# An instance normalization rewritten with one program per engine, an on-chip loop over six slots, a halved last tile and an early short write

## The chip, the cores and the metric

The kernel runs on one core of a Trainium2 chip. A core has a matrix engine (PE), a vector engine (DVE), a scalar engine (ACT), GpSimd (POOL), a sequencer that only issues and waits (SP), and 16 DMA engines that they share. The metric is the device time of one execution in microseconds (us), the median over several runs. The profile of one run gives a span about 1.8 us shorter than that time (1247.6 us against 1249.35 us here), because it counts from the first to the last instruction.

## The reference

```python
def reference(x, eps):           # x: (8, 64, 32, 64, 64) float32, standard normal
    mean = np.mean(x, axis=(2, 3, 4), keepdims=True)
    var = np.var(x, axis=(2, 3, 4), keepdims=True)
    return ((x - mean) / np.sqrt(var + eps)).astype(np.float32)
```

There are 512 instances of 131,072 elements. 268.4 MB are read and 268.4 MB written.

## The kernel before

It is written in a tile framework, which inserts the waits and allocates the semaphores. A tile is 128 partitions by 8192 elements, 4 MB, and holds eight instances, each spread over 16 partitions; there are 64 tiles and six buffers. SP loads, ACT stores.

```python
    def load(g):
        t = data_pool.tile([P, F], fp32, name="xt")          # bufs=6
        nc.sync.dma_start(out=t, in_=x_t[g])
        return t

    def compute(t):
        cut = F // 2
        nc.vector.reduce_sum(out=sums[:, 0:1], in_=t[:, :cut], ...)             # L83
        nc.scalar.activation(out=unused[:, cut:], in_=t[:, cut:],               # L86
                             func=Act.Identity, accum_out=sums[:, 1:2])
        nc.tensor.matmul(out=mean_ps, lhsT=avg, rhs=sums, ...)   # sum over 16 partitions
        nc.vector.tensor_reduce(out=neg_mean, in_=mean_ps, negate=True, ...)
        nc.scalar.activation(out=unused, in_=t, func=Act.Square,                # L103
                             bias=neg_mean, accum_out=squares)
        nc.tensor.matmul(out=var_ps, lhsT=avg, rhs=squares, ...)
        nc.scalar.activation(out=std, in_=var_ps, func=Act.Sqrt, bias=eps_t)
        nc.vector.reciprocal(out=scale, in_=std)
        nc.vector.tensor_mul(out=bias, in0=neg_mean, in1=scale)
        nc.vector.tensor_scalar(out=t[:, cut:], ...)             # x*scale+bias, L114
        nc.scalar.activation(out=t[:, :cut], ...)                # the same,    L122
    # ... cut ...
        for g in range(n_tiles):
            t = load(g)
            compute(t)
            nc.scalar.dma_start(out=out_t[g], in_=t)             # L131
```

## Time and profile before

| | value |
|---|---|
| time, median (first three runs) | 1249.35 us (1249.16 to 1250.83) |
| DMA rate in the middle of the run | 433 GB/s |
| 536.9 MB at that rate | about 1240 us |
| ACT busy, DVE busy | 77%, 37% |

The first lines are the head of the page of the kernel before, its DMA slices (each digit is the busy tenths of a fortieth of the span), its DMA queues (q1 carries the loads, q10 the stores, q14 and q8 instruction fetches) and its DMA issues (the last number is the median time from issue to landing).

```profile
span 1247.6 us, 1828 instructions
PE 73.6 (6%) x256; PEld 64.2 (5%) x256; DVE 467.4 (37%) x322; ACT 961.6 (77%) x386; POOL 0.9 (0%) x6
...
DMA  9999999999999999999999999999999999999998
...
q14 instruction: 9, 0.07, 0.0%
q8 instruction: 2, 0.03, 0.0%
...
xt<-in_x_dram SPq DMA_DIRECT2D x64, 4096.0 KB, 53.3
out_dram<-xt ACTq DMA_DIRECT2D x64, 4096.0 KB, 45.2
```

The DMA engines are busy throughout. A 4 MB tile takes 9.7 us at 433 GB/s if nothing else moves, and a load and a store together take 19.4 us. That transfers need 45 to 53 us to land therefore means that two to three of each kind are always queued. A compute step of a middle tile, which takes ACT about 17.5 us, is hidden.

The windows view of the kernel before gives, for each stretch of the span, its length, the busy time and number of instructions of PE, PE weight loads, DVE, ACT and POOL, the granted clock, the DMA share and the rate in GB/s.

```profile
20.00:40.00 20.00, 1.17 (x4) 1.00 (x4) 7.22 (x5) 18.10 (x8) 0.00 (x0) 1.00 1.00 416
40.00:1200.00 1160.00, 69.58 (x242) 60.68 (x242) 444.97 (x304) 910.77 (x366) 0.00 (x0) 1.00 1.00 433
...
1232.00:1234.00 2.00, 0.00 (x0) 0.00 (x0) 0.00 (x0) 1.15 (x1) 0.00 (x0) 1.00 0.34 147
1234.00:1243.00 9.00, 0.00 (x0) 0.00 (x0) 0.00 (x0) 0.00 (x0) 0.00 (x0) 1.00 1.06 455
1243.00:1246.00 3.00, 0.00 (x0) 0.00 (x0) 0.00 (x0) 0.00 (x0) 0.00 (x0) 1.00 0.15 66
```

For 93% of the span the rate is 433 GB/s. What can be gained lies in the edges: some 416 GB/s where the first store joins, a dip at 1233 us, and a last stretch in which only a few DMA engines still work (share 0.15). The timeline of the kernel before (start, duration, engine, line, what, and in brackets the idle time before it) shows where the dip comes from:

```profile
0.81 75.23 SPq L77 DMA_DIRECT2D xt<-in_x_dram  x8
...
13.07 3.62 ACT L86 ACTIVATE unused<-xt 128x4096 uint8<-128x4096 f32 x1 [10.99 <-DMA xt<-in_x_dram]
...
31.60 0.37 ACTq L131 DMA_DIRECT2D out_dram<-xt  x1
...
1213.72 0.34 ACTq L131 DMA_DIRECT2D out_dram<-xt  x1
...
1229.35 3.80 ACT L122 ACTIVATE xt<-xt,bias,scale 128x4096 f32<-128x4096 f32 x1 [0.47 <-DVE bias L113]
1233.18 0.34 ACTq L131 DMA_DIRECT2D out_dram<-xt  x1
```

The last store can be issued only at 1233.18, about when the store before it, issued at 1213.72, runs dry.

### The profile page before, as it was taken

What the parts mean: (1) busy time and instruction counts of PE and PEld (TensorE: products, weight loads), DVE (VectorE), ACT (ScalarE), POOL (GpSimd) and SP (SyncE); (2) the same over time, 40 slices, a digit from 0 to 9 for tenths busy, and PEclk for the clock granted to TensorE, in tenths of its full rate; (3) what the DMA queues carried; (4) which work ended last, traced back from release to release, by engine and by line L of the source; (5) the groups of instructions that cost most, each with busy time, mean ns of one, the idle gap of its engine ahead of it and who ended that gap; (6) DMA issues with size and microseconds to landing.
All of it is one profiled execution on the core that took longest, in us unless ns stands there. A gap on an engine that the chain in (4) does not pass through costs nothing.

```text
span 1247.6 us, 1828 instructions
## 1 busy us (share of the span) xinstructions
PE 73.6 (6%) x256; PEld 64.2 (5%) x256; DVE 467.4 (37%) x322; ACT 961.6 (77%) x386; POOL 0.9 (0%) x6
## 2 busy tenths in 40 slices
PE   0000000000000000000000000000000000000000
PEld 0000000000000000000000000000000000000000
DVE  2344433433334334343343433434334333343331
ACT  5888888787777877778777777777787777877774
POOL 0000000000000000000000000000000000000000
DMA  9999999999999999999999999999999999999998
GB/s 403 420 437 434 434 427 436 435 435 427 435 436 434 434 428 435 435 434 427 437 435 434 433 429 437 435 432 427 437 436 434 429 431 435 436 434 425 437 436 364
DMA packets 18443, 536.99 MB, mean 430 GB/s; under 512 B 2048, under 2 KB 2048, under 8 KB 2048
## 3 DMA queue, kind: packets, MB, share of 16 engines
q1 hardware_dynamic: 9216, 268.44, 49.9%
q10 hardware_dynamic: 9216, 268.44, 49.8%
q14 instruction: 9, 0.07, 0.0%
q8 instruction: 2, 0.03, 0.0%
HBM read 268.44 MB, written 268.44 MB: 430 GB/s over the span
## 4 chain that ended last, share of the span: by engine, by line
ACT 45%; DVE 32%; another core or an unknown queue 12%; PE 6%; issue 2%; DMA 1%; ACTq 0%
ACT unused L103 37%; DVE sums L83 19%; DVE xt L114 10%; ACT xt L122 4%; ACT unused L86 3%; PE var_ps L107 3%; PE mean_ps L93 3%; ACT std L109 1%; DMA xt<-in_x_dram 1%; DVE scale L111 1%; DVE neg_mean L95 1%; DVE bias L113 1%; ACTq L131 0%; ACT L109 0%
## 5 line engine op out<-in xcount | busy, mean ns | idle before, releaser
L103 ACT ACTIVATE unused<-xt,neg_mean 128x8192 uint8<-128x8192 f32 x64 | 455.8, 7121 | 100.6 <-DVE neg_mean L95 100.6
L83 DVE TENSOR_REDUCE sums<-xt 128x1 f32<-128x4096 f32 x64 | 282.8, 4419 | 167.6 <-DMA xt<-in_x_dram 167.6
L86 ACT ACTIVATE unused<-xt 128x4096 uint8<-128x4096 f32 x64 | 231.5, 3617 | 96.1 <-DMA xt<-in_x_dram 91.5
L122 ACT ACTIVATE xt<-xt,bias,scale 128x4096 f32<-128x4096 f32 x64 | 243.3, 3801 | 31.3 <-DVE bias L113 31.3
L111 DVE RECIPROCAL scale<-std 128x1 f32<-128x1 f32 x64 | 10.5, 164 | 530.8 <-ACT std L109 530.8
L114 DVE TENSOR_SCALAR xt<-xt,scale,bias 128x4096 f32<-128x4096 f32 x64 | 154.4, 2413 | 2.7 <-DVE bias L113 0.3
L93 PE MATMUL mean_ps<-sums,avg 128*128 128x2 f32 x128 | 36.0, 351 | 670.9 <-DVE sums L83 573.9
L93 PEld LDWEIGHTS mean_ps<-sums,avg 128*128 128x128 f32 x128 | 32.1, 311 | 674.7 <-ACT unused L86 657.1
L107 PE MATMUL var_ps<-squares,avg 128*128 128x1 f32 x128 | 37.6, 363 | 484.1 <-ACT unused L103 484.1
L107 PEld LDWEIGHTS var_ps<-squares,avg 128*128 128x128 f32 x128 | 32.1, 312 | 489.6 <-ACT unused L103 489.6
L109 ACT ACTIVATE std<-var_ps,eps_t 128x1 f32<-128x1 f32 x64 | 16.7, 261 | 42.7 <-PE var_ps L107 42.7
L95 DVE TENSOR_REDUCE neg_mean<-mean_ps 128x1 f32<-128x2 f32 x64 | 10.2, 160 | 60.1 <-PE mean_ps L93 60.1
L103 ACT ACTIVATION_READ_ACCUMULATOR unused<-xt,neg_mean 128x1 f32 x64 | 11.9, 187 | 0.0
L86 ACT ACTIVATION_READ_ACCUMULATOR unused<-xt 128x1 f32 x64 | 11.9, 186 | 0.0
L113 DVE TENSOR_TENSOR bias<-neg_mean,scale 128x1 f32<-128x1 f32 x64 | 10.2, 160 | 2.2
L86 ACT ACT_TABLE_LOAD x1 | 1.3, 1283 | 0.8 <-PEq L148 0.8
L109 ACT ACT_TABLE_LOAD x1 | 1.3, 1283 | 0.0
L50 DVE MEMSET avg<- 128x128 f32 x1 | 0.2, 165 | 0.9 <-PEq L148 0.9
L51 POOL TENSOR_SCALAR_AFFINE_SELECT avg<-avg 128x128 f32<-128x128 f32 x1 | 0.3, 343 | 0.6 <-DVE eps_t L71 0.6
L60 POOL TENSOR_SCALAR_AFFINE_SELECT avg<-avg 128x128 f32<-128x128 f32 x1 | 0.3, 338 | 0.1
L148 POOL MEMSET const-bfloat16-1.0<- 128x1 bf16 x1 | 0.1, 102 | 0.0
L148 POOL MEMSET const-uint8-127<- 128x1 uint8 x1 | 0.1, 102 | 0.0
(3 smaller groups left out, 0.3 us busy)
## 6 DMA issues: line engine op xcount, KB each, us to landing
xt<-in_x_dram SPq DMA_DIRECT2D x64, 4096.0 KB, 53.3
out_dram<-xt ACTq DMA_DIRECT2D x64, 4096.0 KB, 45.2
```

Source lines behind the costliest of these rows:

```text
L51: nc.gpsimd.affine_select(out=avg, in_=avg, pattern=[[-SPLIT, IPT], [0, SPLIT]], compare_op=Alu.is_ge, fill=0.0, base=0, channel_multiplier=1,
L83: nc.vector.reduce_sum(out=sums[:, 0:1], in_=t[:, :cut], axis=mybir.AxisListType.X)
L86: nc.scalar.activation(out=unused[:, cut:], in_=t[:, cut:], func=Act.Identity, accum_out=sums[:, 1:2],)
L93: nc.tensor.matmul(out=mean_ps, lhsT=avg, rhs=sums, start=True, stop=True)
L95: nc.vector.tensor_reduce(out=neg_mean, in_=mean_ps, axis=mybir.AxisListType.X, op=Alu.add, negate=True,)
L103: nc.scalar.activation(out=unused, in_=t, func=Act.Square, bias=neg_mean, accum_out=squares)
L107: nc.tensor.matmul(out=var_ps, lhsT=avg, rhs=squares, start=True, stop=True)
L109: nc.scalar.activation(out=std, in_=var_ps, func=Act.Sqrt, bias=eps_t)
L111: nc.vector.reciprocal(out=scale, in_=std)
L113: nc.vector.tensor_mul(out=bias, in0=neg_mean, in1=scale)
L114: nc.vector.tensor_scalar(out=t[:, cut:], in0=t[:, cut:], scalar1=scale, scalar2=bias, op0=Alu.mult, op1=Alu.add,)
L122: nc.scalar.activation(out=t[:, :cut], in_=t[:, :cut], func=Act.Identity, scale=scale, bias=bias)
```

## The change

The intent has four parts. Each engine gets its own program with its own semaphores, one set per lane. Each program is a loop over six slots that stays on the chip, so its code holds the steps of six tiles in the loop and of three tiles and two halves after it, instead of 64. The last tile is processed as two halves of four instances, so that its first half is stored while the second is computed. And a 64 KB write to the output goes out ahead of all loads, to take the cost of the first write off the later stream. The work per tile and the split between ACT and DVE do not change. The diff, cut:

```diff
-    def load(g):
-        t = data_pool.tile([P, F], fp32, name="xt")
-        nc.sync.dma_start(out=t, in_=x_t[g])
+    ctx.enter_context(tc.tile_critical(name="norm"))
+    slots = [sbuf(f"slot{s}", [P, COLS]) for s in range(SLOTS)]
+    landed = semaphores("landed", LANES)        # one per lane; ten more such lists
+    stored = semaphores("stored", LANES)
     # ... cut: on_vector, on_scalar, on_tensor issue the same operations, each with
     # ... an explicit wait, e.g. ._wait_ge(landed[lane], c16).then_inc(summed[lane], 1)
+    for h in range(2):                          # the last tile, in halves
+        k = 2 * (n_tiles - 1) + h
+        half = slots[last][:, h * COLS // 2 : (h + 1) * COLS // 2]
+        rest.append((x_h[k], out_h[k], half, SLOTS + h, 1, FULL // 2))
+        with eng.Fori(0, ROUNDS) as it:         # ROUNDS = 10
+            for s in range(SLOTS):              # SLOTS = 6
+                more = (out_t[it * SLOTS + s],) if with_target else ()
+                step(eng, slots[s][:], s, FULL, *counts, *more)
+    block = ctx.enter_context(nc.Block())
+    @block.scalar
+    def _(eng):
+        eng.dma_start(out=out_t[0][:, 0:128], in_=first[:])._wait_ge(
+            primed, 1
+        ).then_inc(opened, 16)
+        eng.wait_ge(opened, 16)
+        eng.wait_ge(ready, READY)
+        over_tiles(eng, on_scalar, with_target=True)
```

More of the change, by code (lines that the diff above doesn't have):

```diff
@@ L26 @@
     eps_f = float(eps)
-    SPLIT = 16
-    IPT = P // SPLIT
-    F = n_elem // SPLIT
-    n_tiles = n_inst // IPT
+    COLS = 8192
     SLOTS = 6
-    x_t = x.rearrange("b c d h w -> (b c) (d h w)").rearrange(
-        "(k i) (s f) -> k (i s) f", i=IPT, s=SPLIT
-    )
-    out_t = out.rearrange("b c d h w -> (b c) (d h w)").rearrange(
-        "(k i) (s f) -> k (i s) f", i=IPT, s=SPLIT
-    )
-    singles = ctx.enter_context(tc.tile_pool(name="singles", bufs=1))
-    data_pool = ctx.enter_context(tc.tile_pool(name="data", bufs=SLOTS))
@@ L43 @@
-    stat_pool = ctx.enter_context(tc.tile_pool(name="stats", bufs=4))
-    psum_pool = ctx.enter_context(
-        tc.tile_pool(name="psum", bufs=2, space=bass.MemoryType.PSUM)
-    )
-    avg = singles.tile([P, P], fp32, name="avg")
-    nc.vector.memset(avg, 1.0 / n_elem)
-    nc.gpsimd.affine_select(
-        out=avg,
-        in_=avg,
-        pattern=[[-SPLIT, IPT], [0, SPLIT]],
-        compare_op=Alu.is_ge,
-        fill=0.0,
-        base=0,
-        channel_multiplier=1,
-    )
-    nc.gpsimd.affine_select(
-        out=avg,
-        in_=avg,
-        pattern=[[SPLIT, IPT], [0, SPLIT]],
-        compare_op=Alu.is_ge,
-        fill=0.0,
-        base=SPLIT - 1,
-        channel_multiplier=-1,
-    )
@@ L70 @@
-    eps_t = singles.tile([P, 1], fp32, name="eps_t")
-    nc.vector.memset(eps_t, eps_f)
-    unused = singles.tile([P, F], mybir.dt.uint8, name="unused")
-    def load(g):
-        t = data_pool.tile([P, F], fp32, name="xt")
-        nc.sync.dma_start(out=t, in_=x_t[g])
-        return t
-    def compute(t):
-        cut = F // 2
-        sums = stat_pool.tile([P, 2], fp32, name="sums")
-        nc.vector.reduce_sum(
-            out=sums[:, 0:1], in_=t[:, :cut], axis=mybir.AxisListType.X
-        )
-        nc.scalar.activation(
-            out=unused[:, cut:],
-            in_=t[:, cut:],
-            func=Act.Identity,
-            accum_out=sums[:, 1:2],
-        )
-        mean_ps = psum_pool.tile([P, 2], fp32, name="mean_ps")
-        nc.tensor.matmul(out=mean_ps, lhsT=avg, rhs=sums, start=True, stop=True)
-        neg_mean = stat_pool.tile([P, 1], fp32, name="neg_mean")
-        nc.vector.tensor_reduce(
-            out=neg_mean,
-            in_=mean_ps,
+    FULL = P * COLS // n_elem
@@ new lines @@
+    n_tiles = n_inst // FULL
+    ROUNDS = (n_tiles - 1) // SLOTS
+    LANES = SLOTS + 2
+    x_f = x.rearrange("b c d h w -> (b c) (d h w)")
+    out_f = out.rearrange("b c d h w -> (b c) (d h w)")
+    x_t = x_f.rearrange("(k i) (s f) -> k (i s) f", i=FULL, s=P // FULL)
+    out_t = out_f.rearrange("(k i) (s f) -> k (i s) f", i=FULL, s=P // FULL)
+    x_h = x_f.rearrange("(k i) (s f) -> k (i s) f", i=FULL // 2, s=2 * P // FULL)
+    out_h = out_f.rearrange("(k i) (s f) -> k (i s) f", i=FULL // 2, s=2 * P // FULL)
@@ new lines, with sbuf @@
+    ctx.enter_context(tc.tile_critical(name="norm"))
+    def sbuf(name, shape, dtype=fp32):
+        return ctx.enter_context(nc.sbuf_tensor(name, shape, dtype))
+    slots = [sbuf(f"slot{s}", [P, COLS]) for s in range(SLOTS)]
+    unused = sbuf("unused", [P, COLS], mybir.dt.uint8)
+    eps_t = sbuf("eps_t", [P, 1])
+    avg = {n: sbuf(f"avg{n}", [P, P]) for n in (FULL, FULL // 2)}
+    small = [sbuf(f"small{i}", [P, 8]) for i in range(LANES)]
+    psum = [
+        ctx.enter_context(nc.psum_tensor(f"psum{i}", [P, 512], fp32))
+        for i in range(LANES)
+    ]
@@ new lines, in semaphores @@
+    def semaphores(name, n):
+        return [ctx.enter_context(nc.semaphore(f"{name}{i}")) for i in range(n)]
+    ready, primed, opened = semaphores("start", 3)
+    first = sbuf("first", [P, 128])
+    landed = semaphores("landed", LANES)
+    summed = semaphores("summed", LANES)
+    meaned = semaphores("meaned", LANES)
+    centred = semaphores("centred", LANES)
+    squared = semaphores("squared", LANES)
+    varied = semaphores("varied", LANES)
+    rooted = semaphores("rooted", LANES)
+    scaled = semaphores("scaled", LANES)
@@ L98, in compute, with on_vector @@
+    shifted = semaphores("shifted", LANES)
+    done = semaphores("done", LANES)
+    stored = semaphores("stored", LANES)
+    def on_vector(eng, t, lane, n, c1, c2, c16):
+        w = t.shape[1] // 2
+        a = small[lane]
+        eng.reduce_sum(
+            out=a[:, 0:1], in_=t[:, :w], axis=mybir.AxisListType.X
+        )._wait_ge(landed[lane], c16).then_inc(summed[lane], 1)
+        eng.tensor_reduce(
+            out=a[:, 2:3],
+            in_=psum[lane][:, 0:2],
             axis=mybir.AxisListType.X,
@@ L100, in compute @@
             negate=True,
-        )
-        squares = stat_pool.tile([P, 1], fp32, name="squares")
-        nc.scalar.activation(
-            out=unused, in_=t, func=Act.Square, bias=neg_mean, accum_out=squares
-        )
-        var_ps = psum_pool.tile([P, 1], fp32, name="var_ps")
-        nc.tensor.matmul(out=var_ps, lhsT=avg, rhs=squares, start=True, stop=True)
-        std = stat_pool.tile([P, 1], fp32, name="std")
-        nc.scalar.activation(out=std, in_=var_ps, func=Act.Sqrt, bias=eps_t)
@@ L110, in compute @@
-        scale = stat_pool.tile([P, 1], fp32, name="scale")
-        nc.vector.reciprocal(out=scale, in_=std)
-        bias = stat_pool.tile([P, 1], fp32, name="bias")
-        nc.vector.tensor_mul(out=bias, in0=neg_mean, in1=scale)
-        nc.vector.tensor_scalar(
-            out=t[:, cut:],
-            in0=t[:, cut:],
-            scalar1=scale,
-            scalar2=bias,
+        )._wait_ge(meaned[lane], c1).then_inc(centred[lane], 1)
+        eng.reciprocal(out=a[:, 5:6], in_=a[:, 4:5])._wait_ge(
+            rooted[lane], c1
+        ).then_inc(scaled[lane], 1)
@@ L119, in compute @@
+        eng.tensor_mul(out=a[:, 6:7], in0=a[:, 2:3], in1=a[:, 5:6])._wait_ge(
+            scaled[lane], c1
+        ).then_inc(shifted[lane], 1)
+        eng.tensor_scalar(
+            out=t[:, w:],
+            in0=t[:, w:],
+            scalar1=a[:, 5:6],
+            scalar2=a[:, 6:7],
             op0=Alu.mult,
             op1=Alu.add,
-        )
-        nc.scalar.activation(
-            out=t[:, :cut], in_=t[:, :cut], func=Act.Identity, scale=scale, bias=bias
-        )
-    with tc.manual_schedule():
-        for g in range(n_tiles):
-            t = load(g)
-            compute(t)
-            nc.scalar.dma_start(out=out_t[g], in_=t)
+        )._wait_ge(shifted[lane], c1).then_inc(done[lane], 1)
@@ new lines, in on_scalar @@
+    def on_scalar(eng, t, lane, n, c1, c2, c16, dst):
+        w = t.shape[1] // 2
+        a = small[lane]
+        eng.activation(
+            out=unused[:, w : 2 * w],
+            in_=t[:, w:],
+            func=Act.Identity,
+            accum_out=a[:, 1:2],
+        )._wait_ge(landed[lane], c16).then_inc(summed[lane], 1)
+        eng.activation(
+            out=unused[:, : 2 * w],
+            in_=t,
+            func=Act.Square,
+            bias=a[:, 2:3],
+            accum_out=a[:, 3:4],
+        )._wait_ge(centred[lane], c1).then_inc(squared[lane], 1)
+        eng.activation(
+            out=a[:, 4:5], in_=psum[lane][:, 2:3], func=Act.Sqrt, bias=eps_t[:, 0:1]
+        )._wait_ge(varied[lane], c1).then_inc(rooted[lane], 1)
+        eng.activation(
+            out=t[:, :w],
+            in_=t[:, :w],
+            func=Act.Identity,
+            scale=a[:, 5:6],
+            bias=a[:, 6:7],
+        )._wait_ge(shifted[lane], c1).then_inc(done[lane], 1)
+        eng.dma_start(out=dst, in_=t)._wait_ge(done[lane], c2).then_inc(
+            stored[lane], 16
+        )
@@ new lines, in on_tensor @@
+    def on_tensor(eng, t, lane, n, c1, c2, c16):
+        a = small[lane]
+        eng.matmul(
+            out=psum[lane][:, 0:2],
+            lhsT=avg[n][:],
+            rhs=a[:, 0:2],
+            start=True,
+            stop=True,
+        )._wait_ge(summed[lane], c2).then_inc(meaned[lane], 1)
+        eng.matmul(
+            out=psum[lane][:, 2:3],
+            lhsT=avg[n][:],
+            rhs=a[:, 3:4],
+            start=True,
+            stop=True,
+        )._wait_ge(squared[lane], c1).then_inc(varied[lane], 1)
@@ new lines, with over_tiles @@
+    rest = [
+        (x_t[k], out_t[k], slots[k % SLOTS][:], k % SLOTS, k // SLOTS + 1, FULL)
+        for k in range(ROUNDS * SLOTS, n_tiles - 1)
+    ]
+    last = (n_tiles - 1) % SLOTS
+    for h in range(2):
+        k = 2 * (n_tiles - 1) + h
+        half = slots[last][:, h * COLS // 2 : (h + 1) * COLS // 2]
+        rest.append((x_h[k], out_h[k], half, SLOTS + h, 1, FULL // 2))
+    def over_tiles(eng, step, with_target=False):
+        counts = [
+            ctx.enter_context(eng.register(f"{step.__name__}_c{m}")) for m in (1, 2, 16)
+        ]
+        for c, m in zip(counts, (1, 2, 16)):
+            eng.reg_mov(c, m)
+        with eng.Fori(0, ROUNDS) as it:
+            for s in range(SLOTS):
+                more = (out_t[it * SLOTS + s],) if with_target else ()
+                step(eng, slots[s][:], s, FULL, *counts, *more)
+            for c, m in zip(counts, (1, 2, 16)):
+                eng.reg_add(c, c, m)
+        for _, dst, t, lane, c, n in rest:
+            more = (dst,) if with_target else ()
+            step(eng, t, lane, n, c, 2 * c, 16 * c, *more)
@@ new lines @@
+    block = ctx.enter_context(nc.Block())
+    @block.sync
+    def _(eng):
+        for s in range(SLOTS):
+            eng.dma_start(out=slots[s][:], in_=x_t[s]).then_inc(landed[s], 16)
+        c16 = ctx.enter_context(eng.register("load_c16"))
+        eng.reg_mov(c16, 16)
+        with eng.Fori(1, ROUNDS) as it:
+            for s in range(SLOTS):
+                eng.dma_start(out=slots[s][:], in_=x_t[it * SLOTS + s])._wait_ge(
+                    stored[s], c16
+                ).then_inc(landed[s], 16)
+            eng.reg_add(c16, c16, 16)
+        for src, _, t, lane, c, n in rest:
+            behind = lane if lane < SLOTS else last
+            uses = c - 1 if lane < SLOTS else ROUNDS
+            eng.dma_start(out=t, in_=src)._wait_ge(stored[behind], 16 * uses).then_inc(
+                landed[lane], 16
+            )
@@ new lines, in _ @@
+    @block.gpsimd
+    def _(eng):
+        count = 0
+        for n, m in avg.items():
+            split = P // n
+            eng.memset(m[:], 1.0 / n_elem).then_inc(ready, 1)
+            count += 1
+            for sign in (-1, 1):
+                eng.affine_select(
+                    out=m[:],
+                    in_=m[:],
+                    pattern=[[sign * split, n], [0, split]],
+                    compare_op=Alu.is_ge,
+                    fill=0.0,
+                    base=0 if sign < 0 else split - 1,
+                    channel_multiplier=-sign,
+                )._wait_ge(ready, count).then_inc(ready, 1)
+                count += 1
+        eng.memset(eps_t[:], eps_f).then_inc(ready, 1)
@@ new lines, with _ @@
+    READY = 3 * len(avg) + 1
+    @block.vector
+    def _(eng):
+        eng.memset(first[:], 0.0).then_inc(primed, 1)
+        over_tiles(eng, on_vector)
+    @block.tensor
+    def _(eng):
+        eng.wait_ge(ready, READY)
+        over_tiles(eng, on_tensor)
+    @block.scalar
+    def _(eng):
+        eng.dma_start(out=out_t[0][:, 0:128], in_=first[:])._wait_ge(
+            primed, 1
+        ).then_inc(opened, 16)
+        eng.wait_ge(opened, 16)
+        eng.wait_ge(ready, READY)
+        over_tiles(eng, on_scalar, with_target=True)
+        for s in range(SLOTS):
+            uses = ROUNDS + sum(1 for r in rest if r[3] == s)
+            eng.wait_ge(stored[s], 16 * uses)
+        for s in range(SLOTS, LANES):
+            eng.wait_ge(stored[s], 16)
```

## The prediction

> **What bounds it now.** The 16 DMA engines. The page's slices show them 9 tenths busy from end to end, while ACT, the busiest compute engine, has 77%. The Trainium skill, "DMA: Bandwidth & Descriptors", section Specifications, gives 435 GB/s as the fabric ceiling; the windows view shows 433 GB/s from 39.6 to 1213.8 us, which agrees, and 536.9 MB at 433 GB/s is 1239.3 us of the 1247.6 us span. The chain of waits, which names ACT and DVE lines, misleads: loads take 53 us and stores 45 us to land (DMA issues), so two to three transfers of each kind are always queued and no compute step of a middle tile sets the time.
>
> So only about 8.3 us are to be had, by the trace's packet records:
> - first byte at 1.8 us;
> - the first packets take about 2 us instead of 1.213: 0.75 us per engine;
> - when the first store joins at 34 us packets take 1.4 to 2.0 us: 0.65 us (403 GB/s in the window 20 to 39.6);
> - a gap of 0.8 us at 1233, between the stores of tiles 62 and 63, on 14 of 16 engines;
> - 11 instruction fetches (the page's instruction queues), 8 or 16 KB, each holding up one DMA engine 0.5 to 0.7 us. ACT needs five, 245 us apart, all on one DMA engine. Twelve engines finish near 1243.8, the others at 1244.5, 1244.8, 1245.4 and 1246.3, which fits one, two, three and five fetches. The last ends the kernel; it has no gap at 1233;
> - completion and closing barrier 1.3 us.
>
> **What the change does.** Engine work per tile is the same; two activation table loads (1.28 us each) return in every loop pass of six tiles, off the critical path, since ACT has 1.9 us spare per 19.4 us tile. The loops shrink each program, so most mid-run fetches should go: up to 2.5 us at the end. Halving the last tile removes the gap: the second half's store should issue near 1234.8 (10.4 us of serial work per half, estimated from the page's means), while the first half's store keeps the engines busy to 1237. Alone this gains nothing, as the slowest engine had no gap; with the fetches gone it counts. The short write should move the first-store hold-up to the start, where packets are slow anyway: 0.4 to 0.6 us gained, 0.2 us paid. Nothing makes the loads wait for it. The extra blocks and barriers cost about 0.4 us before the first load and 0.5 us at the end (guesses from the order of barriers).
>
> Sum: 1249.35 − 2.5 − 0.6 + 0.2 + 0.4 + 0.5 = about 1247.3 us.
>
> **Prediction.** 1247.3 us, range 1244.5 to 1251.5. Faster by over 2%: 0.01; within 2%: 0.97; slower: 0.02.
>
> **What would show each step.** The middle stays at 433 GB/s. Packets of the instruction queues fall from 11 to a few; the DMA engines finish within 1 us of each other. No window below 430 GB/s around 34 us, none around 1233. The last store issues near 1235, half as large.
>
> **What would make it wrong.** The ACT loop ends, as I count, about where its first 8 KB of instructions end. The Trainium skill, "Runtime: NRT & Kernel Launch", section Instruction fetch mechanics, says that a taken branch out of the two-page window forces a fetch. If every pass refetches, ten passes with one or two fetches put 5 to 14 us on one DMA engine: 1252 to 1260 us. No run shows this yet. Or the hold-up comes anyway with the first large store, or the halves end late and leave a gap.

## The result, and the profile after

| | before | after |
|---|---|---|
| time, median of four runs | 1249.38 us | 1249.18 us |
| all runs | 1249.16 to 1250.83 | 1249.09 to 1249.24 |
| ratio | | 0.9996, 95% interval 0.9979 to 1.0013 |

A ratio here is the mean time of one kernel's fast runs over that of the other's of the same rounds, so it is not quite the ratio of the medians. The time is the same. The head of the page, the queue and the issues of the changed kernel:

```profile
span 1247.5 us, 1822 instructions
...
q14 instruction: 2, 0.02, 0.0%
...
slot<-in_x_dram SPq DMA_DIRECT2D x63, 4096.0 KB, 46.1
out_dram<-slot ACTq DMA_DIRECT2D x63, 4096.0 KB, 52.6
...
out_dram<-first ACTq DMA_DIRECT2D x1, 64.0 KB, 14.7
```

Instruction fetches fell from 11 to 2, as intended. The short write needed 14.7 us to land: the loads were already queued, and it shared the DMA engines with them. The windows of the changed kernel:

```profile
20.00:40.00 20.00, 1.76 (x6) 1.50 (x6) 7.23 (x6) 17.56 (x9) 0.00 (x0) 1.00 1.00 418
40.00:1200.00 1160.00, 71.63 (x244) 61.20 (x244) 444.88 (x306) 940.62 (x385) 0.00 (x0) 1.00 1.00 433
...
1232.00:1234.00 2.00, 0.00 (x0) 0.00 (x0) 0.00 (x0) 0.00 (x0) 0.00 (x0) 1.00 1.01 434
1234.00:1243.00 9.00, 0.00 (x0) 0.00 (x0) 0.00 (x0) 0.00 (x0) 0.00 (x0) 1.00 0.99 426
1243.00:1246.00 3.00, 0.00 (x0) 0.00 (x0) 0.00 (x0) 0.00 (x0) 0.00 (x0) 1.00 0.07 27
```

The middle is at the same 433 GB/s. The dip at 1233 us is gone (434 GB/s instead of 147). Windows of 2 us are rough here, since a packet of 1.2 us counts whole in the window in which it starts (shares above 1 come from that). Counted by the starts and ends of the packets, each of the 16 engines idled 0.77 us on average between 1215 and 1242.5 us before, and 0.01 us after. Yet there is still a stretch after 1243 us in which little moves: 0.07 of 16 engines is about one engine. The timeline of the changed kernel:

```profile
1.03 2.99 SPq L184 DMA_DIRECT2D slot<-in_x_dram  x6
...
1.32 0.42 ACTq L237 DMA_DIRECT2D out_dram<-first  x1
...
16.29 1.28 ACT L108 ACT_TABLE_LOAD   x1 [16.29 <-DMA out_dram<-first]
17.58 3.62 ACT L108 ACTIVATE unused<-slot 128x4096 uint8<-128x4096 f32 x1
...
35.20 0.36 ACTq L131 DMA_DIRECT2D out_dram<-slot  x1
...
1219.53 0.34 ACTq L131 DMA_DIRECT2D out_dram<-slot  x1
...
1230.89 0.34 ACTq L131 DMA_DIRECT2D out_dram<-slot  x1
```

SP issues its first load at 1.03 and ACT the write at 1.32, so the write is not ahead of the loads. ACT waits for it until 16.29 and starts its first tile 4.5 us later than before. The last store is issued at 1230.89, 2.3 us earlier and half as large.

**Where the difference lies.** A transfer raises its semaphore 16 times, once for each DMA engine that is done with its share (the Trainium skill, "DMA: Bandwidth & Descriptors", section Why a DMA increments its semaphore by 16 and not by 1, says so, and the traces show 16 landings for each 128-partition transfer). The landing records thus show, without naming an engine, how late each one is. The span splits into these terms:

| us | before | after | difference |
|---|---|---|---|
| last transfer landed on the median engine | 1244.21 | 1243.53 | −0.68 |
| latest engine behind the median | 2.60 | 2.41 | −0.19 |
| last landing to the end of the span | 0.83 | 1.55 | +0.72 |
| span | 1247.64 | 1247.49 | −0.15 |

The DMA side gained 0.87 us, and the longer closing (barriers of the block and of the framework around it) took 0.72 us back. And one DMA engine ends each kernel alone. In the changed kernel this engine does not fall behind in steps, as it would with fetches, but evenly (until about 340 us the latest is another engine, so the table shows its drift only after that):

```
landing of a load or store at (us)      85   202   395   511   705   899  1092  1243.5
latest engine behind the median        0.31  0.46  0.42  0.73  1.16  1.62  2.04  2.41
second latest                          0.13  0.27  0.34  0.36  0.32  0.35  0.35  0.98
```

I followed this engine through the trace's packet records, backwards from the last packet. Of its 994 packets since 59 us, 357 took a few to some 30 ns more than the usual 1213 ns. These excesses sum to 2.40 us, which is its lag. (The records do not name the engine, so the chain is ambiguous where packets of two engines end together; a second way of chaining, which lost the engine before about 340 us, found 262 long packets and 1.88 us. Six of the other engines had none in 995 packets.) The long packets contained, on average, 0.52 ends of matmuls, the normal ones 0.09 (0.46 and 0.14 in the second chaining, from 376 us on); for most short instructions of ACT and DVE the ratio was three to four. That pointed to the compute engines' activity.

### The profile page after: what moved, and what is told of

Read it like the earlier page. It is cut to its first block, busy times and chain, and to the rows that moved or that the text cites. A ratio compares the mean times of both kernels' runs of the same rounds, so it can differ in the third digit from the quotient of the medians.

```text
span 1247.5 us, 1822 instructions
## 1 busy us (share of the span) xinstructions
PE 76.3 (6%) x260; PEld 65.2 (5%) x260; DVE 467.6 (37%) x326; ACT 986.1 (79%) x410; POOL 1.9 (0%) x11
## 4 chain that ended last, share of the span: by engine, by line
another core or an unknown queue 62%; ACT 22%; DMA 9%; PE 2%; DVE 1%; SPq 1%; issue 1%; ACTq 0%; DVEq 0%
ACT unused L114 10%; ACT slot L124 5%; ACT unused L108 5%; DMA out_dram<-slot 4%; DMA slot<-in_x_dram 4%; SPq L189 1%; DMA out_dram<-first 1%; PE psum L137 1%; PE psum L144 1%; DVE small L80 1%; ACTq L131 0%; ACT small L121 0%; ACT L121 0%; ACT L108 0%
## 5 line engine op out<-in xcount | busy, mean ns | idle before, releaser
L114 ACT ACTIVATE unused<-slot,small 128x8192 uint8<-128x8192 f32 (+1 forms) x65 | 456.1, 7016 | 87.3 <-DVE small L83 87.3
L80 DVE TENSOR_REDUCE small<-slot 128x1 f32<-128x4096 f32 (+1 forms) x65 | 282.9, 4352 | 151.7 <-DMA slot<-in_x_dram 151.7
L108 ACT ACTIVATE unused<-slot 128x4096 uint8<-128x4096 f32 (+1 forms) x65 | 231.7, 3564 | 69.0 <-DMA slot<-in_x_dram 62.6
L124 ACT ACTIVATE slot<-slot,small 128x4096 f32<-128x4096 f32 (+1 forms) x65 | 243.7, 3749 | 27.6 <-DVE small L93 27.6
L96 DVE TENSOR_SCALAR slot<-slot,small 128x4096 f32<-128x4096 f32 (+1 forms) x65 | 154.7, 2380 | 2.4
L137 PE MATMUL psum<-small,avg 128*128 128x2 f32 x130 | 38.1, 363 | 671.2 <-DVE small L80 498.4
L137 PEld LDWEIGHTS psum<-small,avg 128*128 128x128 f32 x130 | 32.5, 311 | 676.7 <-DVE small L80 502.4
L144 PE MATMUL psum<-small,avg 128*128 128x1 f32 x130 | 38.2, 363 | 480.5 <-ACT unused L114 480.5
L144 PEld LDWEIGHTS psum<-small,avg 128*128 128x128 f32 x130 | 32.7, 313 | 486.1 <-ACT unused L114 486.1
L121 ACT ACTIVATE small<-psum,eps_t 128x1 f32<-128x1 f32 x65 | 17.0, 261 | 37.4 <-PE psum L144 37.3
L108 ACT ACTIVATION_READ_ACCUMULATOR unused<-slot 128x1 f32 x65 | 12.1, 186 | 0.0
## 6 DMA issues: line engine op xcount, KB each, us to landing
out_dram<-first ACTq DMA_DIRECT2D x1, 64.0 KB, 14.7
```

The lines of the kernel that those rows point to most:

```text
L80: eng.reduce_sum(out=a[:, 0:1], in_=t[:, :w], axis=mybir.AxisListType.X)._wait_ge(landed[lane], c16).then_inc(summed[lane], 1)
L96: eng.tensor_scalar(out=t[:, w:], in0=t[:, w:], scalar1=a[:, 5:6], scalar2=a[:, 6:7], op0=Alu.mult, op1=Alu.add,)._wait_ge(shifted[lane], ...
L108: eng.activation(out=unused[:, w : 2 * w], in_=t[:, w:], func=Act.Identity, accum_out=a[:, 1:2],)._wait_ge(landed[lane], c16).then_inc(sum ...
L114: eng.activation(out=unused[:, : 2 * w], in_=t, func=Act.Square, bias=a[:, 2:3], accum_out=a[:, 3:4],)._wait_ge(centred[lane], c1).then_in ...
L121: eng.activation(out=a[:, 4:5], in_=psum[lane][:, 2:3], func=Act.Sqrt, bias=eps_t[:, 0:1])._wait_ge(varied[lane], c1).then_inc(rooted[lane ...
L124: eng.activation(out=t[:, :w], in_=t[:, :w], func=Act.Identity, scale=a[:, 5:6], bias=a[:, 6:7],)._wait_ge(shifted[lane], c1).then_inc(don ...
```

## The experiments

Twelve runs in three sets; the sets ran on three chips, with the kernel before beside each (medians 1249.56, 1249.57 and 1249.44 us). The kernel before has single longer runs (up to 1256.66 us), which widen the intervals of the ratios; the changed kernels repeat within 0.2 to 0.5 us mostly, so I also compare their medians.

Theory A: the end is set by one DMA engine, late for a reason of its own, and most of what the change improves happens on the others. Theory B: the parts work as intended, and new barriers take the gain back.

### The changed kernel again

> The changed kernel unaltered, as the reference for the runs beside it. Theory A (one late engine): one of the 16 DMA engines again falls behind the median of the others by about 2.4 us, evenly from about 100 us on, and ends the kernel; if that engine is a property of the chip it may be absent or different here. Theory B (the savings were real but were paid back in new barriers, 0.25 us at the start and 0.7 us at the end): the engines end together and only the barriers are long. Expected 1249.2 us, within 0.3 us.

1249.21 us (1249.14 to 1249.30), latest engine 2.44 us behind. The late engine and its lag reproduce on another run.

### Without the short write

```diff
-        eng.dma_start(out=out_t[0][:, 0:128], in_=first[:])._wait_ge(
-            primed, 1
-        ).then_inc(opened, 16)
-        eng.wait_ge(opened, 16)
```

> The changed kernel without the short write and without ACT's wait for it. Theory A and B: the write buys nothing, since in the trace of the changed kernel packets were still held up (0.6 us per engine) just before the first large store; so without it the time is the same within 0.3 us (about 1249.0), the first ACT instruction on a tile starts about 4 us earlier, and the hold-up stays 0.6 us. The write's intent (it takes the first-store hold-up off the later stream): 0.5 us or more slower, with a larger hold-up.

1248.56 us (1248.39 to 1248.75): 0.65 us faster than with the write, with no overlap of the runs. The expectation was 0.2 us, so this was a small miss. ACT began its first tile at 13.36 instead of 17.53 us. Packets were held up around the first large store (their time over 1213 ns, summed over all packets from 10 to 60 us and divided by 16 engines) by 0.67 us per engine without the write, and by 0.58 and 0.66 us in the two traces with it: the write did not take the hold-up away. Without the write the last transfer landed 0.22 us earlier on the median engine and the lag of the late engine was 2.12 instead of 2.44 us. The first term fits the write's own packets; why the lag shrank was not tested. What the hold-up itself is stays open.

### With the last tile whole

```diff
-    for h in range(2):
-        k = 2 * (n_tiles - 1) + h
-        half = slots[last][:, h * COLS // 2 : (h + 1) * COLS // 2]
-        rest.append((x_h[k], out_h[k], half, SLOTS + h, 1, FULL // 2))
+    k = n_tiles - 1
+    rest.append((x_t[k], out_t[k], slots[last][:], SLOTS, 1, FULL))
```

> The changed kernel with the last tile whole. Theory A: a gap of about 0.8 us returns between the last two stores on 15 of the 16 DMA engines, but the late engine, 2.4 us behind, has none, so the time is the same within 0.3 us (1249.2). The prediction's view and Theory B (halving removes a gap that counts once the fetches are gone): 0.8 us or more slower, about 1250.0.

1249.33 us (1249.33 to 1249.47), 0.12 us slower than with halves. The halving is worth next to nothing in this program. But the gap that every theory expected to return did not: the last store was issued at 1228.34 us, before the one ahead of it ran dry, and the engines idled 0.00 us between 1215 and 1242.5 us. So the run does not test what halving buys where there is a gap; Theory A has its time right, and its reason untested. What moved the store forward is open. The latest engine was 2.41 us behind. The last transfer even landed 0.15 us earlier than with halves (1245.78 against 1245.93 us); the closing was longer (1.85 against 1.55 us).

### With the loops written out

```diff
-        with eng.Fori(0, ROUNDS) as it:
+        for it in range(ROUNDS):
             for s in range(SLOTS):
-                step(eng, slots[s][:], s, FULL, *counts, *more)
+                step(eng, slots[s][:], s, FULL, it + 1, 2 * it + 2, 16 * it + 16, *more)
```

> The changed kernel with its loops written out, waits on constants. Instruction fetches should be back at about 11. Theory A: only the one fetch that falls on the late engine counts, 0.65 us more, about 1249.8; ACT's five put another engine about 2.9 us behind, still not last. The prediction's view (ACT's five fetches set the end): 2.5 us more, about 1251.7. No difference at all would say that fetches never reach the end.

1249.40 us (1249.31 to 1249.76) with 9 fetches in the span and 369 instructions fewer, only 0.19 us slower than the loop with 2. The fetches show: five engines now end 1.26 to 2.23 us behind the median, where in the changed kernel only one is over 1 us. But none of them ends later than the late engine of the changed kernel did (2.41 and 2.44 us). So 2.5 us as the gain of looping is excluded. Theory A's 0.65 us was too much as well. But the run does not isolate the fetches: it changes the number of instructions too. Followed through its packets, the engine that ends last here carries three fetches (174.4, 653.3 and 1151.5 us) and hardly drifts, so it is not the evenly falling engine of the loop. And the last transfer landed 0.16 us earlier than in the loop (1245.77 against 1245.93 us); the 0.19 us lie in the closing (1.83 against 1.55 us).

### Fifteen DMA engines for the last stores

To relieve engine 15, if it was the late one, each half was stored without it (on top of the kernel without the write):

```diff
+            eng.dma_start(out=dst[120:], in_=t[120:])._wait_ge(done[lane], c2)...
+            eng.dma_start(out=dst[:120], in_=t[:120]).then_inc(stored[lane], 16)
```

> As the run without the short write (1248.56 us), but each half of the last tile is stored in two pieces: 8 partitions first, then 120 partitions. The Trainium skill's DMA page says that the count of DMA engines divides the outermost dimension, so 120 partitions would use engines 0 to 14 and 8 partitions engines 0 to 7, which leaves engine 15 without work in the last 4 MB. Theory A with the late engine being engine 15: it finishes some 2.1 us earlier, the others about 1.2 us later at most, and the time falls 0.7 to 1.5 us, to about 1247.4. Theory A with the late engine among 0 to 14: 1.2 us more, about 1249.8. No late engine at all: 0.6 to 1.2 us more.

1254.21 us (1253.52 to 1254.82), 5.6 us slower: worse than every theory said. A 120-partition transfer did end on 15 engines at different times (the sixteenth increment of its semaphore came at once), but unevenly: its 15 landings spread from 1244.64 to 1251.47 us, single 16 KB packets took up to 3.46 us (median 0.61), and issuing the second one took 3.57 us instead of 0.34. Which engine is late this run cannot tell. Why such a transfer is uneven was not followed up.

### Without the framework's barriers

```diff
-    ctx.enter_context(tc.tile_critical(name="norm"))
...
-    with _tile.TileContext(nc) as tc:
-        tile_instance_norm_3d_kernel(tc, *args)
+    tile_instance_norm_3d_kernel(_Holder(nc), *args)     # only hands nc over
```

(and without the short write)

> As the run without the short write (1248.56 us), but without the tile framework around the block: one pair of barriers less at the start and the end. Theory B, the part on barriers: first load issued 0.2 us earlier (0.8 instead of 1.03) and 0.4 to 0.5 us less from the last landing to the end, so about 1247.9 us. If barriers are not what the 1.5 us after the last landing consist of, no change.

1247.16 us (1247.09 to 1247.26). Run again with five rounds:

> The same kernel as the run without write and without the tile framework's barriers (1247.16 us, where the kernel before had an outlier that left the interval wide), with five rounds for a narrower interval. Expected 1247.1 to 1247.3 us and a ratio to the kernel before of 0.998, interval within 0.997 to 0.999.

1247.26 us (1247.10 to 1247.46), ratio to the kernel before 0.9978, interval 0.9965 to 0.9991: 0.2% faster. The runs of the changed kernel, in other sets, all lie above 1249 us. The first byte moved at 1.83 us instead of 2.04, and the end came 0.49 us after the last landing instead of 1.54, more than I had expected. This is Theory B's part, confirmed: 0.2 us at the start and 1.05 us at the end were barriers. In its windows, too, only a few engines still work after 1243 us:

```profile
1232.00:1234.00 2.00, 0.00 (x0) 0.00 (x0) 1.02 (x1) 1.77 (x1) 0.00 (x0) 1.00 0.71 303
1234.00:1243.00 9.00, 0.00 (x0) 0.00 (x0) 0.00 (x0) 0.00 (x0) 0.00 (x0) 1.00 0.95 408
1243.00:1246.00 3.00, 0.00 (x0) 0.00 (x0) 0.00 (x0) 0.00 (x0) 0.00 (x0) 1.00 0.04 16
```

One engine again ended last, 2.17 us behind the median. The last store comes later here (1233.80 us), and the 2 us window reads 303 GB/s. That is no gap but the coarse count described above: by their starts and ends, the packets left the engines idle for 0.01 us between 1215 and 1242.5 us.

### No compute at all

Loads and stores only, on top of the kernel without the write:

> Wrong result on purpose: loads and stores of the run without the short write, no compute at all. Theory A1 (the late engine's packets are lengthened by what the compute engines do, since in the trace the long packets of that engine contain five times as many instruction ends as its normal ones): with a quarter of the instructions the lag falls from 2.1 us to 0.5 us or less and the time by 1.5 to 2 us, to about 1246.8. Theory A2 (that DMA engine is slower in itself): the lag stays near 2 us and the time at 1248.3 or more. The stores begin at about 14 us in both.

1248.05 us (1247.92 to 1248.13): 0.5 us faster than with all the compute, not the 1.5 to 2 us expected. The lag of the latest engine fell from 2.12 to 1.05 us, in the direction of Theory A1 but not to 0.5; the median engine's last landing was 0.5 us later. Of that, 0.2 us is a gap near 1238 us (423 GB/s from 1232 to 1242 us); the rest was not followed. The plain lesson of this run is that all the compute of this kernel costs 0.5 us. The check of results passed this copy, although I had meant it as a wrong result: the input is standard normal, so it is nearly its own normalization, and a passing result says little in this case.

### More instructions on an idle engine

```diff
+                eng.wait_ge(landed[s], c16)
+                for i in range(20):
+                    eng.memset(first[:, i : i + 1], 0.0).then_inc(primed, 1)
```

> As the run without the short write (1248.56 us), with 1200 tiny memsets of 0.1 us on the idle POOL engine, 20 as each tile lands. They touch no tile and nothing waits for them. Theory A1 (lag follows the number of instructions, by the trace about 1.1 ns for each): the late engine lags by 3.5 to 4 us instead of 2.1, time 1250 to 1250.5. Theory A2 (slow in itself) or a lag that only DMA traffic causes: no change, 1248.6.

1252.17 us (1251.88 to 1252.42), 3.6 us slower, although POOL is otherwise idle and nothing waits for it. Its page head and last windows:

```profile
span 1250.3 us, 3092 instructions
...
1243.00:1246.00 3.00, 0.00 (x0) 0.00 (x0) 0.00 (x0) 0.00 (x0) 0.00 (x0) 1.00 0.10 44
1246.00:1252.00 6.00, 0.00 (x0) 0.00 (x0) 0.00 (x0) 0.00 (x0) 0.00 (x0) 1.00 0.02 8
```

The median engine's last landing was at 1243.57 us, 0.3 us later than without the memsets; the latest engine was 5.20 us behind it instead of 2.12, again growing evenly (0.81 us at 326, 2.60 at 635, 5.24 at 1139 us). So 1200 small instructions put 3.1 us on one DMA engine, about 2.6 ns each, more than the 1.1 ns I had put down. That such instructions, which touch no tile, lengthen the lag is shown by this run together with the next, whose POOL program has the same loop and the same waits for the loads but no memsets. Theory A2 falls as the whole cause; the 1.05 us of lag that remain without any compute are not explained.

### What about the instruction counts

```diff
-                    eng.memset(first[:, i : i + 1], 0.0).then_inc(primed, 1)
+                    eng.reg_add(cx, cx, 1)
```

> As the run without the short write (1248.56 us), with 20 register additions on the idle POOL sequencer as each tile lands, 1200 in all, in place of the 1200 memsets that made it 1252.17 us and the late engine 5.2 us late. They touch no memory and raise no semaphore. Theory C1 (what lengthens the late engine's packets is the number of instructions that a sequencer carries out, whatever they are): the lag is again about 5 us and the time about 1252. Theory C2 (it is writes to memory or semaphore increments by compute engines): the lag stays near 2.1 us and the time at 1248.6.

1248.75 us, lag 1.95 us, no change. This does not decide between C1 and C2: the trace has only 83 POOL instructions, because the build folded the additions into a few, so the dose never arrived. It does show that the loop and its waits alone leave the lag as it was.

```diff
-        with eng.Fori(1, ROUNDS) as it:            # SP, with addresses in registers
+        for it in range(1, ROUNDS):                # SP, constants
```

> As the previous one, with the load loop of SP alone written out: no address arithmetic and no branch, about 130 instructions fewer of 1779. Theory A1 (lag follows the instruction count, 2.4 ns each by the run with memsets): the late engine 0.3 us less late, time about 1246.9. If SP's longer program needs one more instruction fetch and that falls on the late engine, as in the kernel before, 0.3 us more instead, about 1247.5.

(on top of the kernel without the framework's barriers.) 1247.23 us, five of six runs 1247.06 to 1247.31 and one at 1249.49; the same as with the loop (1247.26), with 130 instructions fewer. The lag was 1.76 us, against 1.86 and 2.17 us in the two traces of the loop, so within their scatter. The expected 0.3 us did not show in the time. Memsets that write memory and raise a semaphore lengthened packets; for register and address arithmetic nothing shows it. Which of the memset's actions does it is open, and so is whether the recording of the trace takes part: every run lists a span, so all were recorded.

### The kernel before with a halved last tile

The tile framework's kernel with its last tile loaded, computed and stored in halves:

```diff
+        t = data_pool.tile([P, F], fp32, name="xt")
+        halves = [t[:, h * F // 2 : (h + 1) * F // 2] for h in range(2)]
+        for h, part in enumerate(halves):
+            nc.sync.dma_start(out=part, in_=x_h[2 * (n_tiles - 1) + h])
+        for h, part in enumerate(halves):
+            compute(part, avgs[2 * SPLIT])
+            nc.scalar.dma_start(out=out_h[2 * (n_tiles - 1) + h], in_=part)
```

> The kernel before with its last tile in two halves and nothing else. Theory A: no gain, since the DMA engine that ends last had no gap to fill: within 0.4 us of the kernel before (1249.4), while the gap at 1233 us is gone on the other engines. The prediction said the same of halving alone. A rival (halving pays in itself): 0.8 us or more faster.

1257.24 us (1256.39 to 1257.70), ratio 1.0057, interval 1.0043 to 1.0072: 8 us slower, which nobody had expected. The timeline of this run:

```profile
1131.95 3.80 ACT L134 ACTIVATE xt<-xt,bias,scale 128x4096 f32<-128x4096 f32 x1 [0.48 <-DVE bias L125]
1137.32 4.42 DVE L95 TENSOR_REDUCE sums<-xt 128x1 f32<-128x4096 f32 x1 [3.01 <-DMA xt<-in_x_dram]
1156.77 0.34 ACTq L143 DMA_DIRECT2D out_dram<-xt  x1
1157.16 3.62 ACT L98 ACTIVATE unused<-xt 128x4096 uint8<-128x4096 f32 x1 [21.40 <-DMA xt<-in_x_dram]
```

ACT finishes a tile at 1135.75 but can issue its store only at 1156.77. In the semaphore records that store waits for semaphore 106, which a load issued at 1104.65 also raises: the framework hands a few semaphores to loads and stores in turn, and the extra load shifts the turn so that a store waits for an unrelated load. ACT then works at 17.5 us per tile and has no time left to catch up; the last store is issued at 1248.09. The changed kernel has a semaphore of its own per lane and no such stall; giving the framework's kernel one was not tried.

## Why the prediction was right or wrong

The predicted time was 1247.3 us, range 1244.5 to 1251.5, and "within 2%". 1249.18 us lies in the range, but of the 2.05 us that the sum forecast, 0.2 us came. The range held "no change" (1249.35 us) as well, so that the time fell into it says nothing for the sum. Point by point:

- **Bound by the DMA engines, at 433 GB/s in the middle: right.** Both windows show it, and the copy (1248.05 us) shows that removing all the compute gains 0.5 us.
- **"most mid-run fetches should go: up to 2.5 us at the end": this step failed.** The fetches went (11 to 2), but looping gained about 0.2 us (loops written out, 1249.40 us, a run that changes the instructions too). I had read the 1243.8, 1244.5, 1244.8, 1245.4 and 1246.3 us at which engines end as none, one, two, three and five fetches. It was a fit of four numbers without following an engine through time. Followed, the last engine falls behind evenly in both kernels; in the kernel before it fell back about 0.11 us every 38.7 us (0.09 in the changed one), and had one step of about 0.7 us between landings at 519 and 558 us, where SP's only fetch (524.7 us) lies. ACT's five fetches (122.0, 359.8, 604.7, 857.0 and 1102.1 us) lie among the packets of another engine, the one that ended 1.58 us behind the median, 1.0 us before the last. (Whose fetch each one is, is inferred; the records do not name it.) Removing them freed an engine that was not last. On the last engine lay one fetch instead of five, 0.7 us instead of 2.5. The last transfer did land 0.87 us earlier in the changed kernel, which is near that size, but no run removes this fetch alone.
- **"Halving … alone this gains nothing, … with the fetches gone it counts": not shown.** The gap went, but in the changed kernel it is absent with the tile whole too, so closing it did not need the halving. That the last engine had no gap the trace of the kernel before does show: from the last store but one to the last, its lag behind the median fell from 3.82 to 2.60 us, because the others waited and it did not. And alone, in the framework, halving lost 8 us through shared semaphores, which I had not looked for. The half's serial work was estimated at 10.4 us and took 10.5 us (store issue 1230.89 minus start 1220.44); the last store came 3.9 us before the estimated 1234.8.
- **The short write "0.4 to 0.6 us gained, 0.2 us paid": wrong.** It was not ahead of the loads, it did not remove the hold-up (0.66 us after, 0.70 us before), and removing it gained 0.65 us.
- **Extra blocks and barriers 0.4 us at the start and 0.5 us at the end: right in sum.** The first byte came 0.25 us later, and the closing took 0.72 us more, 0.97 us together.
- **The feared refetch in every pass did not come.** Only two fetches were left.

So the forecast gain was lost in two places: most of the fetches, and the gap, were not on the last engine, and the short write cost 0.65 us where a gain was forecast. The barriers cost about what was forecast. Without the write and the framework's barriers the program is at 1247.26 us.

## What to carry to other kernels

When DMA bounds a kernel, look at when each DMA engine ends, not at the mean share: savings on engines that are not last are not savings, and an engine has to be followed through time before its lateness is put down to a cause. Count the barriers, waits and setup that a rewrite adds at its two edges as carefully as what it removes. And before splitting a transfer in a framework that shares semaphores, look which unrelated transfer a store will then wait for.

## What the Trainium skill lacked or had wrong

- "DMA: Bandwidth & Descriptors", section Latency and other measured facts, says that DMA engines 7 and 15 are usually slower and gives software descriptor rings as its best guess at the cause. Here all bulk transfers ran on SP's and ACT's hardware queues, and one engine (not identified) still fell 2.1 to 2.4 us behind in 1245 us. No page says that such a lag depends on what the compute engines do: with 1200 more tiny memsets it was 5.2 us, with no compute 1.05 us.
- "Runtime: NRT & Kernel Launch", section Instruction fetch mechanics, speaks of 16 KiB blocks. The kernel before fetched 8,192 bytes nine times and 16,384 bytes twice. It calls the cost "mostly hidden" and does not speak of the DMA engine that fetches, which a fetch made about 0.5 to 0.7 us late. Its warning about branches did not apply: ten loop passes left two fetches.
- "DMA: Bandwidth & Descriptors", section Why a DMA increments its semaphore by 16 and not by 1, gives the number of DMA engines for a transfer but not that 15 of them can be much slower: the last 120-partition transfer ended 6.8 us apart on its engines, and the run was 5.6 us slower.
- No page has the hold-up of about 0.6 us per engine when the first large store joins running loads; a 64 KB write beforehand did not prevent it.
